# Feature-major products: all matmuls on a unit's high weights ahead of those on its low weights

## The chip, the cores and the metric

The kernel runs on one core of one Trainium2 chip. The metric is the device time of one execution in microseconds (us); the median of the runs counts. One core has TensorE (matrix products, called PE in the profile, its weight loads PEld), VectorE (DVE), ScalarE (ACT), GpSimd (POOL) and SyncE (SP, which here issues most transfers).

## The reference, cut to what matters

Two transformer layers follow one another on 256 tokens of 2048 features, all in float32.

```python
# first layer
proj = rmsnorm(x, norm_mix) @ w_in          # q, k, v of two attentions, and two gates
merged = sigmoid(ga) * (out_a @ w_branch_a) + sigmoid(gb) * (out_b @ w_branch_b)
x = x + merged @ w_out
u = rmsnorm(x, norm_ffn) @ w_up             # 2 x 5632 columns, then a convolution over three tokens
x = x + (silu(gate) * val) @ w_down
# second layer
h = rms_norm(x, g_norm) * (1 + scale) + shift
proj = h @ w_in_2                           # two more attentions, one with a choice of keys
x = x + gate * (concat([ya * silu(za), yb * silu(zb)]) @ w_out_2)
```

Nearly all of the arithmetic lies in the products with the weight matrices, some 395 MB of weights that are read once.

## The kernel before

A float32 product is made of three products in float32r, a shorter form of float32 that TensorE takes at a higher rate. Weights and activations are each split in two parts: `hi` is the value rounded to float32r and `lo` is what is left. The product is hi times hi, hi times lo and lo times hi.

**The stream of weights.** `Plan` writes down the order of all weight blocks. SP loads each block into a tile `raw`. A block is cut into units of 1024 numbers on each of the 128 partitions. For each unit ACT makes `wh` (high part, line 262) and DVE makes `wl` (low part, line 263), four buffers of each; `take` hands the next unit to a product and has the split of the unit three ahead put into the queues. `take` also lets the work beside the stream (`pump`: attention, norms, sums of finished products) put one step into the queues. The whole program is written out ahead of time; each engine works through its own queue in that order, and waits on semaphores where it needs another's result.

**Two kinds of product.** `gemm_tok` holds a tile of activations as TensorE's stationary matrix and streams a tile of weights, 512 columns (some 464 or 384) through it, lines 342 to 344: three matmuls of that width for each tile of 128 features and each half of the tokens. `gemm_feat` is the other way round: a tile of 128 x 128 weights is stationary and the activations of 256 tokens stream through. There `both` is the high and the low part of the activations side by side, 512 columns, so that one matmul on `wh` (line 368, here called wide) does two of the three products, and one on `wl` with the high part alone (line 369, 256 columns, called narrow) does the third. The left halves and the right halves of the result are added later (`sum_pair`, `grow`).

Each matmul has a weight load of its own in front of it, also where the stationary matrix is the same as before.

**Units in a feature-major product.** A unit holds four feature tiles of two column tiles each (f = 0, 1), or two feature tiles of four column tiles each. Both are eight pairs of a wide and a narrow matmul. A few products are made with `one=True`: there the low part of the activations is added in the same 256 columns, so that a unit is eight triples of 256-column matmuls, lines 365, 366 and 369. These are the first three chunks of the FFN's up product (8 + 4 + 4 units), the last chunk of its last down product (3 units) and the last chunk of the second layer's output product (4 units).

`ensure` is a hook that, before the tile k is used, has the instructions written that produce it, where a product starts while its activations are still being made.

Of the kernel before, what the change touches and what calls it, by code (L numbers as in the profile page):

```python
# [15 lines left out]
P = 128  # L16
# [26 lines left out]
class Paged:  # L43
    """A tensor of [128, 256] parts, four to a page; a page is taken at its first use."""

# [16 lines left out]
class Split:  # L62
    """A tensor of [128, 256] parts, each as two float32r parts side by side; two to a page."""

# [28 lines left out]
class Ahead:  # L93
    """Feature tiles built by a generator, per tiles at a step: a hook of a product over k, lead tiles ahead of it."""

# [17 lines left out]
class Plan:  # L113
    """The weights in the order in which they are used: blocks of [nk * 128, ncol], each one load, each cut into
    units of work."""

# [35 lines left out]
    def plan_ada(self, j):  # L152
        """128 columns of the modulation's matrix, turned: [columns, 2048]."""
        i = len(self.specs)
        self.block("w_ada_2", 0, 2, j, 1024)
        self.units.append((i, 0, 1, False))
        self.ada_half.append((i, 1, 1, True))
# [50 lines left out]
class Prog:  # L208
# [24 lines left out]

# [1 line left out]
    def issue_dma(self, upto):  # L235
# [41 lines left out]

# [1 line left out]
    def page(self, name, dtype=F32):  # L279
# [16 lines left out]

# [1 line left out]
    def pump(self):  # L298
# [28 lines left out]

# [1 line left out]
    def gemm_tok(self, a, nk, ncol, ensure=None):  # L329
        """[tokens, columns] as a tile [128, half, columns]."""  # L330
        nc = self.nc
        ps = self.mm()
        k = 0
        while k < nk:
            hv, lv, n = self.take(lambda: ensure(k) if ensure is not None else None)
            for j in range(n):
                if ensure is not None:
                    ensure(k)
                for t in range(2):
                    aH, aL = a(k, t)  # L340
                    o = ps[:, t, :ncol]
                    nc.tensor.matmul(o, aH, hv[:, j], start=(k == 0), stop=False)  # L342
                    nc.tensor.matmul(o, aH, lv[:, j], start=False, stop=False)  # L343
                    nc.tensor.matmul(o, aL, hv[:, j], start=False, stop=(k == nk - 1))  # L344
                k += 1
        return ps

    def gemm_feat(self, a, nk, ensure=None, nf=2, one=False):
        """[columns, tokens]; each pair of column tiles as (tile, tile) of [128, 512], to be summed by halves;
        one: summed already, in the first halves."""  # L350
        nc = self.nc
        mm = self.mm()
        ps = [mm[:, f] if f < 2 else self.sp() for f in range(nf)]
        k = 0
        while k < nk:
            hv, lv, n = self.take(lambda: ensure(k) if ensure is not None else None)
            for j in range(n):
                if ensure is not None:
                    ensure(k)
                both, hi, lo = a(k)  # L360
                for f in range(nf):
                    wH, wL = hv[:, j, f * P:(f + 1) * P], lv[:, j, f * P:(f + 1) * P]
                    first, last = k == 0, k == nk - 1
                    if one:
                        nc.tensor.matmul(ps[f][:, :256], wH, hi, start=first, stop=False)  # L365
                        nc.tensor.matmul(ps[f][:, :256], wH, lo, start=False, stop=False)  # L366
                    else:
                        nc.tensor.matmul(ps[f], wH, both, start=first, stop=False)  # L368
                    nc.tensor.matmul(ps[f][:, :256], wL, hi, start=False, stop=last)  # L369
                k += 1  # L370
        return [mm] + ([ps[2:]] if nf > 2 else [])

    def sum_pair(self, ps, out=None):
        """The sum of the two halves of the products of a pair; yields once, then the sum."""
        nc = self.nc
        lo = self.w2("lo").rearrange("p (f c) -> p f c", f=2)
        if isinstance(ps, list):
            for f in range(2):
                nc.scalar.copy(lo[:, f], ps[f][:, 256:])
        else:  # L380
            nc.scalar.copy(lo, ps[:, :, 256:])  # L381
        yield
        if out is None:
            out = lo
        if isinstance(ps, list):
            for f in range(2):
                nc.vector.tensor_tensor(out=out[:, f], in0=ps[f][:, :256], in1=lo[:, f], op=ALU.add)
        else:
            nc.vector.tensor_tensor(out=out, in0=ps[:, :, :256], in1=lo, op=ALU.add)
        yield out  # L390

# [1 line left out]
    def rsqrt_mean(self, out, ssq, n, width):  # L393
# [8 lines left out]

# [1 line left out]
    def load_x(self, g, steps=(4,), between=None):  # L404
# [14 lines left out]
    def square(self, i):  # L419
        """Squares of one pair of feature tiles, added up over the pairs; the last pair by itself."""  # L420
        nc = self.nc
        two = lambda t: t.rearrange("p (k c) -> p k c", k=2)
        if i == 0:
            nc.scalar.activation(two(self.ssum), self.xpair(0), AF.Square)
            return
        sq = self.w2("sqx")
        if i == 7:
            x = self.xpair(i)
            nc.scalar.activation(two(sq)[:, 0], x[:, 0], AF.Square)
            nc.vector.tensor_tensor(out=two(sq)[:, 1], in0=x[:, 1], in1=x[:, 1], op=ALU.mult)  # L430
            self.slast = sq
            return
        nc.scalar.activation(two(sq), self.xpair(i), AF.Square)  # L433
        nc.gpsimd.tensor_tensor(out=self.ssum, in0=self.ssum, in1=sq, op=ALU.add)  # L434
        if i == 6:
            nc.gpsimd.tensor_tensor(out=self.ssum[:, :256], in0=self.ssum[:, :256], in1=self.ssum[:, 256:], op=ALU.add)

    def token_sums(self, first):
        """Sums over the features of the squares of each token, [tokens, 1] for each half: all pairs but the last,
        then the last."""  # L440
        if first:
# [21 lines left out]
    def token_rstd(self):  # L463
        """1 / rms of each token: rtok [tokens, half] and rbc [every partition, token]."""
        self.token_sums(True)
# [23 lines left out]
    def build_raw(self, h, gain):  # L489
        """h = x * gain, without 1 / rms; yields after each feature tile."""  # L490
        for k in range(KD):
# [10 lines left out]
    def build_scaled(self, h, gain):  # L502
        """h = x * rstd * gain; yields after each pair of feature tiles."""
        nc = self.nc
# [11 lines left out]
    def build_shifted(self, h, gain, shift, r):  # L516
        """h = x * rstd * gain + shift; yields after each pair of feature tiles."""
        nc = self.nc
# [31 lines left out]
    def catch_up(self, gen, nk):  # L550
        """A hook of the product that reads what gen writes last, as its last two tiles."""
        def ensure(k):
# [6 lines left out]
    def grow(self, i, ps, h=None, gain=None, last=True, one=False):  # L559
        """x += product of one pair of feature tiles; squares summed and h = x * gain when it is the last addend."""  # L560
        nc = self.nc
# [22 lines left out]
    def heads(self, ps, t, runs, wait=0, rt=None):  # L584
        """One half of the tokens of one chunk: heads normed, turned, transposed; values copied.
        runs: (kind, first column, heads, destination, gain, rope)"""
        nc = self.nc
# [55 lines left out]
    def run_of(self, i, n, q, k, v, nq, nk, gq, gk, rq=None, rk=None, col=0):  # L643
        """Heads i .. i+n of the row q(nq) k(nk) v as runs; no run crosses a page."""
        out = []
# [28 lines left out]
    def attend(self, q, k, v, bias, emit, sink=None, causal=False):  # L674
        """softmax(q k + bias) v of one head, all queries; q, k: [d, tokens]; v(kt): [tokens, d].
        causal: the first half of the queries takes the first half of the keys only."""
        nc = self.nc
# [77 lines left out]

# [1 line left out]
    def ada_step(self, j, half, raw):  # L757
# [20 lines left out]

# [1 line left out]
    def run(self):  # L780
# [202 lines left out]
    def ffn(self):  # L983
# [17 lines left out]
        def conv_pair(ps, f, by):  # L1001
            """Yields between the engines; the last value is the pair of convolved tiles."""
            if by:
# [343 lines left out]
```

## Time and profile before

| what | value |
|---|---|
| time, median of 3 runs | 1910.98 us (1908.72 to 1911.16) |
| span of the profiled execution, first to last instruction | 1909.2 us |
| PE busy | 1890.8 us (99%) |
| DVE busy | 1372.0 us (72%) |
| ACT busy | 995.6 us (52%) |
| bytes moved | 399.07 MB, 209 GB/s on average |
| granted TensorE clock, mean of the span | 0.995 |

The profiled execution's own time is its span of 1909.2 us, which lies between the fastest and the slowest of the three runs. A granted clock of 1.00 is 2.4 GHz. Matmuls overlap at their ends: a matmul's duration in a row (0.40 us for a wide one) is longer than the time from its start to the next one's start, so pace is read from starts, or from counts in a stretch.

### The profile page before, as it was taken

What the parts mean: (1) busy time and instruction counts of PE and PEld (TensorE: products, weight loads), DVE (VectorE), ACT (ScalarE), POOL (GpSimd) and SP (SyncE); (2) the same over time, 40 slices, a digit from 0 to 9 for tenths busy, and PEclk for the clock granted to TensorE, in tenths of its full rate; (3) what the DMA queues carried; (4) which work ended last, traced back from release to release, by engine and by line L of the source; (5) the groups of instructions that cost most, each with busy time, mean ns of one, the idle gap of its engine ahead of it and who ended that gap; (6) DMA issues with size and microseconds to landing.
All of it is one profiled execution on the core that took longest, in us unless ns stands there. A gap on an engine that the chain in (4) does not pass through costs nothing.

```text
span 1909.2 us, 26942 instructions
## 1 busy us (share of the span) xinstructions
PE 1890.8 (99%) x10556; PEld 1639.9 (86%) x10556; DVE 1372.0 (72%) x2082; ACT 995.6 (52%) x1449; POOL 103.0 (5%) x87
## 2 busy tenths in 40 slices
PE   8999999999999999999999999999899999999999
PEld 6888888888888988888888888888788888898888
DVE  6888688677787877786777776666656855677664
ACT  6466555555454555533555434554454545666542
POOL 2111000000001300000000000000200100100000
PEclk9999999999999999999999999999899999999999
DMA  8665666666676466586555675454455455454562
GB/s 315 231 219 204 222 215 210 222 238 225 255 272 231 167 223 218 205 314 230 214 206 210 254 289 218 177 191 167 143 197 177 155 199 178 139 185 160 177 215 94
DMA packets 59231, 399.07 MB, mean 209 GB/s; under 512 B 6752, under 2 KB 7520, under 8 KB 14304
## 3 DMA queue, kind: packets, MB, share of 16 engines
q1 hardware_dynamic: 58176, 395.06, 57.4%
q0 software_dynamic: 640, 2.10, 0.3%
q8 instruction: 83, 1.36, 0.3%
q14 instruction: 44, 0.36, 0.0%
q10 hardware_dynamic: 288, 0.19, 0.0%
HBM read 395.22 MB, written 2.10 MB: 208 GB/s over the span
## 4 chain that ended last, share of the span: by engine, by line
PE 97%; DVE 2%; issue 1%; DMA 0%; ACT 0%; POOL 0%; SPq 0%; DVEq 0%; POOLq 0%; ACTq 0%
PE mm L368 42%; PE mm L369 22%; PE mm L342 8%; PE mm L344 8%; PE mm L343 8%; PE s L368 2%; PE s L369 1%; PE t L633 1%; PE t L730 1%; PE mm L365 1%; PE mm L366 1%; DVE h L485 1%; DVE wl L263 0%; DMA x<-in_x_dram 0%; PE t L750 0%
## 5 line engine op out<-in xcount | busy, mean ns | idle before, releaser
L263 DVE TENSOR_TENSOR wl<-raw,wh 128x1024 fp32r<-128x1024 f32 (+2 forms) x649 | 790.5, 1221 | 479.8 <-ACT wh L262 474.7
L262 ACT CAST wh<-raw 128x1024 fp32r<-128x1024 f32 (+2 forms) x649 | 675.1, 1042 | 662.9 <-PE mm L368 399.0
L368 PE MATMUL mm<-h,wh 128*128 128x512 f32 x2176 | 770.5, 398 | 0.0
L369 PE MATMUL mm<-h,wl 128*128 128x256 f32 x2272 | 638.0, 281 | 3.0 <-DVE wl L263 3.0
L368 PEld LDWEIGHTS mm<-h,wh 128*128 128x128 f32 x2176 | 408.8, 188 | 99.1
L369 PEld LDWEIGHTS mm<-h,wl 128*128 128x128 f32 x2272 | 429.4, 189 | 3.5 <-DVE wl L263 3.4
L342 PE MATMUL mm<-wh,h 128*128 128x512 f32 (+2 forms) x704 | 276.9, 393 | 5.0 <-DVE h L542 2.3
L344 PE MATMUL mm<-wh,h 128*128 128x512 f32 (+2 forms) x704 | 272.2, 387 | 3.1 <-DVE h L485 2.4
L343 PE MATMUL mm<-wl,h 128*128 128x512 f32 (+2 forms) x704 | 271.9, 386 | 0.0
L368 PE MATMUL mm<-g,wh 128*128 128x512 f32 x592 | 211.3, 399 | 0.0
L369 PE MATMUL mm<-g,wl 128*128 128x256 f32 x616 | 173.1, 281 | 0.0
L342 PEld LDWEIGHTS mm<-wh,h 128*128 128x128 f32 x704 | 134.6, 191 | 30.4 <-ACT wh L262 2.9
L344 PEld LDWEIGHTS mm<-wh,h 128*128 128x128 f32 x704 | 134.2, 191 | 29.7 <-DVE h L485 3.5
L343 PEld LDWEIGHTS mm<-wl,h 128*128 128x128 f32 x704 | 134.5, 191 | 22.7 <-DVE wl L263 0.6
L368 PEld LDWEIGHTS mm<-g,wh 128*128 128x128 f32 x592 | 111.2, 188 | 27.8
L759 DVE CUSTOM_DVE_ANT_0 raw<-raw,silu_c 128x1024 f32<-128x1024 f32 x96 | 119.2, 1242 | 0.0
L369 PEld LDWEIGHTS mm<-g,wl 128*128 128x128 f32 x616 | 116.4, 189 | 0.0
L381 ACT COPY lo<-mm 128x512 f32<-128x512 f32 x84 | 49.0, 584 | 62.9 <-PE mm L369 58.7
L434 POOL TENSOR_TENSOR ssum<-ssum,sqx 128x512 f32<-128x512 f32 x18 | 27.1, 1503 | 1015.1 <-ACT sqx L433 1014.9
L368 PE MATMUL mm<-m,wh 128*128 128x512 f32 x224 | 79.9, 399 | 0.0
L368 PE MATMUL mm<-y,wh 128*128 128x512 f32 x192 | 67.3, 394 | 0.0
L369 PE MATMUL mm<-m,wl 128*128 128x256 f32 x224 | 62.9, 281 | 0.0
(247 smaller groups left out, 2053.3 us busy)
## 6 DMA issues: line engine op xcount, KB each, us to landing
raw<-in_weights_dram SPq DMA_DIRECT2D x350, 1024.0 KB, 4.8
raw<-in_weights_dram SPq DMA_DIRECT2D x12, 768.0 KB, 4.3
raw<-in_weights_dram SPq DMA_DIRECT2D x11, 512.0 KB, 5.7
raw<-in_weights_dram SPq DMA_DIRECT2D x4, 928.0 KB, 4.6
x<-in_x_dram SPq DMA_DIRECT2D x6, 512.0 KB, 8.3
bias<-in_bias_b_dram POOLq DMA_DIRECT2D x8, 256.0 KB, 3.8
out_dram<-r SPq DMA_DIRECT2D x7, 256.0 KB, 2.0
silu_c<-in_c_dram SPq DMA_DIRECT2D x2, 512.0 KB, 7.4
```

The lines of the kernel that those rows point to most:

```text
L262: nc.scalar.copy(hv, rv)
L263: nc.vector.tensor_tensor(out=lv, in0=rv, in1=hv.bitcast(F32), op=ALU.subtract)
L342: nc.tensor.matmul(o, aH, hv[:, j], start=(k == 0), stop=False)
L343: nc.tensor.matmul(o, aH, lv[:, j], start=False, stop=False)
L344: nc.tensor.matmul(o, aL, hv[:, j], start=False, stop=(k == nk - 1))
L365: nc.tensor.matmul(ps[f][:, :256], wH, hi, start=first, stop=False)
L366: nc.tensor.matmul(ps[f][:, :256], wH, lo, start=False, stop=False)
L368: nc.tensor.matmul(ps[f], wH, both, start=first, stop=False)
L369: nc.tensor.matmul(ps[f][:, :256], wL, hi, start=False, stop=last)
L381: nc.scalar.copy(lo, ps[:, :, 256:])
L434: nc.gpsimd.tensor_tensor(out=self.ssum, in0=self.ssum, in1=sq, op=ALU.add)
L759: nc.vector.tensor_tensor_reduce(out=raw, in0=raw, in1=self.silu_c[half], scale=1.0, scalar=0.0, op0=ALU.mult, op1=ALU.add, accum_out=self ...
```

## The change

In `gemm_feat` the matmuls of a unit are regrouped. Before, a column tile's matmul on the high weights and that on its low weights follow each other, for each feature tile and column tile in turn. Now the loop over the unit's feature tiles does all matmuls on `hv` first, and a second loop does all matmuls on `lv`. The number of matmuls, their operands and their sums stay as they are (up to the order of addition). The hook `ensure(k + j)` of all tiles of a unit now comes before the first matmul on low weights. Lines further down the file move by five (368 becomes 370, 369 becomes 373, 365 and 366 become 367 and 368); apart from that only docstrings and comments differ.

```diff
             hv, lv, n = self.take(lambda: ensure(k) if ensure is not None else None)
+            parts = []
             for j in range(n):
                 if ensure is not None:
-                    ensure(k)
-                both, hi, lo = a(k)
+                    ensure(k + j)
+                parts.append(a(k + j))
+                both, hi, lo = parts[j]
                 for f in range(nf):
-                    wH, wL = hv[:, j, f * P:(f + 1) * P], lv[:, j, f * P:(f + 1) * P]
-                    first, last = k == 0, k == nk - 1
+                    wH = hv[:, j, f * P:(f + 1) * P]
+                    first = k + j == 0
                     if one:
                         nc.tensor.matmul(ps[f][:, :256], wH, hi, start=first, stop=False)
                         nc.tensor.matmul(ps[f][:, :256], wH, lo, start=False, stop=False)
                     else:
                         nc.tensor.matmul(ps[f], wH, both, start=first, stop=False)
-                    nc.tensor.matmul(ps[f][:, :256], wL, hi, start=False, stop=last)
-                k += 1
+            for j in range(n):
+                for f in range(nf):
+                    nc.tensor.matmul(ps[f][:, :256], lv[:, j, f * P:(f + 1) * P], parts[j][1], start=False,
+                                     stop=k + j == nk - 1)
+            k += n
```

**An ordinary unit.** This is TensorE's queue in one unit of the FFN's up product, before; `mm` is the result in PSUM, `h` the activations (two feature tiles to a page), and "waits" names the engines whose semaphores an instruction waits on (Activation is ACT). The unit goes on in this way to its sixteenth matmul.

```order
L368 MATMUL mm_6870<-h_6168,wh_6874 128x512 [waits Activation_49]
L369 MATMUL mm_6870<-h_6168,wl_6875 128x256 [waits DVE_49]
L368 MATMUL mm_6870<-h_6168,wh_6874 128x512
L369 MATMUL mm_6870<-h_6168,wl_6875 128x256
L368 MATMUL mm_6870<-h_6168,wh_6874 128x512
L369 MATMUL mm_6870<-h_6168,wl_6875 128x256
```

The same unit of the changed kernel, whole; x3 and x4 are so many instructions in a row that read alike.

```order
L370 MATMUL mm_6870<-h_6168,wh_6874 128x512 [waits Activation_49]
L370 MATMUL mm_6870<-h_6168,wh_6874 128x512 x3
L370 MATMUL mm_6870<-h_6208,wh_6874 128x512 x4
L373 MATMUL mm_6870<-h_6168,wl_6875 128x256 [waits DVE_49]
L373 MATMUL mm_6870<-h_6168,wl_6875 128x256 x3
L373 MATMUL mm_6870<-h_6208,wl_6875 128x256 x4
```

Eight wide matmuls now stand in a row and eight narrow ones behind them, and the first instruction that waits for `wl` has moved from the second place to the ninth.

**A unit of the products with one sum.** TensorE's queue at the second unit of the third chunk of the FFN's up product, before:

```order
L365 MATMUL mm_6128<-h_5228,wh_6061 128x256 [waits Activation_49]
L366 MATMUL mm_6128<-h_5228,wh_6061 128x256
L369 MATMUL mm_6128<-h_5228,wl_6062 128x256 [waits DVE_49]
L365 MATMUL mm_6128<-h_5228,wh_6061 128x256
L366 MATMUL mm_6128<-h_5228,wh_6061 128x256
L369 MATMUL mm_6128<-h_5228,wl_6062 128x256
```

The end of the same unit's matmuls on `wh` and its matmuls on `wl`, of the changed kernel (fourteen matmuls of lines 367 and 368 stand ahead of these rows):

```order
L367 MATMUL mm_6128<-h_5324,wh_6061 128x256
L368 MATMUL mm_6128<-h_5324,wh_6061 128x256
L373 MATMUL mm_6128<-h_5228,wl_6062 128x256 [waits DVE_49]
L373 MATMUL mm_6128<-h_5228,wl_6062 128x256 x3
L373 MATMUL mm_6128<-h_5324,wl_6062 128x256 x4
```

The wait for `wl` has moved from the unit's third matmul to its seventeenth.

## Rows read from the trace of the kernel before

**Rows 1.** The page's head, busy time, and slices.

```profile
span 1909.2 us, 26942 instructions
PE 1890.8 (99%) x10556; PEld 1639.9 (86%) x10556; DVE 1372.0 (72%) x2082; ACT 995.6 (52%) x1449; POOL 103.0 (5%) x87
...
PEclk9999999999999999999999999999899999999999
```

**Rows 2.** The page's chain that ended last, by engine and by line.

```profile
PE 97%; DVE 2%; issue 1%; DMA 0%; ACT 0%; POOL 0%; SPq 0%; DVEq 0%; POOLq 0%; ACTq 0%
PE mm L368 42%; PE mm L369 22%; PE mm L342 8%; PE mm L344 8%; PE mm L343 8%; PE s L368 2%; PE s L369 1%; PE t L633 1%; PE t L730 1%; PE mm L365 1%; PE mm L366 1%; DVE h L485 1%; DVE wl L263 0%; DMA x<-in_x_dram 0%; PE t L750 0%
```

**Rows 3.** The page's costliest groups: weight splits and token-major matmuls.

```profile
L263 DVE TENSOR_TENSOR wl<-raw,wh 128x1024 fp32r<-128x1024 f32 (+2 forms) x649 | 790.5, 1221 | 479.8 <-ACT wh L262 474.7
...
L342 PE MATMUL mm<-wh,h 128*128 128x512 f32 (+2 forms) x704 | 276.9, 393 | 5.0 <-DVE h L542 2.3
```

**Rows 4.** Windows, instructions of line 368 alone.

```profile
core 0: us, PE busy (x) PEld busy (x), PEclk, DMA share, GB/s
...
900.00:1000.00 100.00, 100.00 (x284) 53.18 (x283) 1.00 0.57 207
...
1800.00:1850.00 50.00, 50.00 (x145) 27.07 (x145) 1.00 0.58 206
1850.00:1910.00 60.00, 43.77 (x127) 23.55 (x126) 0.98 0.32 116
```

**Rows 5.** Timeline of PE, feature-major product at 900 us.

```profile
900.24 0.40 PE L368 MATMUL mm<-h,wh 128*128 128x512 f32 x1
900.47 0.28 PE L369 MATMUL mm<-h,wl 128*128 128x256 f32 x1
900.59 0.40 PE L368 MATMUL mm<-h,wh 128*128 128x512 f32 x1
900.83 0.28 PE L369 MATMUL mm<-h,wl 128*128 128x256 f32 x1
```

**Rows 6.** Timeline of PE, feature-major product at 1820 us.

```profile
1820.23 0.39 PE L368 MATMUL mm<-y,wh 128*128 128x512 f32 x1
...
1833.75 0.40 PE L368 MATMUL s<-y,wh 128*128 128x512 f32 x1
```

**Rows 7.** Timeline of PE, token-major product at 1578 us.

```profile
1578.20 0.39 PE L344 MATMUL mm<-wh,h 128*128 128x512 f32 x1
...
1582.96 0.39 PE L344 MATMUL mm<-wh,h 128*128 128x512 f32 x1
```

**Rows 8.** Timeline of PE, six attention matmuls within a token-major product.

```profile
129.99 0.39 PE L344 MATMUL mm<-wh,h 128*128 128x512 f32 x1
130.21 0.28 PE L748 MATMUL t<-pH,vs 128*128 128x256 f32 x1
130.33 0.28 PE L749 MATMUL t<-pL,vs 128*128 128x256 f32 x1
...
130.93 0.40 PE L342 MATMUL mm<-wh,h 128*128 128x512 f32 x1
131.16 0.40 PE L343 MATMUL mm<-wl,h 128*128 128x512 f32 x1
131.40 0.39 PE L344 MATMUL mm<-wh,h 128*128 128x512 f32 x1
...
132.31 0.39 PE L342 MATMUL mm<-wh,h 128*128 128x512 f32 x1
132.54 0.39 PE L343 MATMUL mm<-wl,h 128*128 128x512 f32 x1
```

**Rows 9.** Timeline of PE, one-sum product, line 369 alone.

```profile
643.62 0.39 PE L369 MATMUL mm<-h,wl 128*128 128x256 f32 x1 [0.54 <-DVE wl L263]
644.09 0.28 PE L369 MATMUL mm<-h,wl 128*128 128x256 f32 x1
...
646.25 0.28 PE L369 MATMUL mm<-h,wl 128*128 128x256 f32 x1
...
652.18 0.39 PE L369 MATMUL mm<-h,wl 128*128 128x256 f32 x1 [2.45 <-DVE wl L263]
```

**Rows 10.** Waits of PE: line, for whom, us in total, times, longest.

```profile
PE mm L369 <- DVE wl L263: 3.0, 2, 2.4
PE mm L344 <- DVE h L485: 2.4, 2, 2.0
```

**Rows 11.** Windows, all engines, around the one-sum products.

```profile
640.00:660.00 20.00, 17.02 (x139) 16.58 (x139) 19.65 (x32) 15.35 (x25) 4.73 (x3) 1.00 0.47 167
```

## Prediction

> **What bounds the kernel now.** I read the page's busy times first, then its chain of work that ended last, then the timeline of TensorE alone, and windows to see over how much of the span a pace holds. TensorE is busy for 99% of the span, no other engine for more than 72%, and the granted clock is 1.00 (2.4 GHz) but for one slice [rows 1]. The chain is 97% PE, and the two lines that the change regroups, 368 and 369, are 64% of it in the main tile alone [rows 2]. So TensorE sets the time, and the change can matter in two ways only: the pace at which TensorE starts its matmuls, and the few places where it waits.
>
> The pace, from start to start. In a feature-major product a wide matmul (512 columns) and its narrow one (256) take together 0.35 us: wide to narrow 0.23 or 0.24, narrow to wide 0.12 [rows 5]. A window says it more sharply: 283 weight loads of line 368 in 100 us, 353.4 ns a pair [rows 4]; I find 283 or 284 in each window of 100 us from 400 to 600 us and from 700 to 1300 us, of which one stands there. Near the end the same code runs at another pace: 39 pairs from 1820.23 to 1833.75, 346.7 ns a pair [rows 6], and so in the last two windows. So there are two paces of the same alternation, 6.7 ns apart.
>
> Now matmuls of one width in a row. Wide behind wide, in a token-major product: 21 steps in 1578.20 to 1582.96, 226.7 ns each [rows 7]. Narrow behind narrow, in the products with one sum: 18 steps in 644.09 to 646.25, 120.0 ns each [rows 9]. Their sum, 346.7, is the faster pace of the alternation. The slower pace is thus what the alternation adds, and it is what there is to win.
>
> One more reading, at which the trace comes nearest to the new order: a run of six narrow attention matmuls between wide ones [rows 8]. The first narrow one behind a wide one is followed after 0.12 us, like the others. But the wide ones behind the run do not fall at once into 0.227: the first starts at 130.93, the next at 131.16, 131.40, and only from 132.31 on do they run as in rows 7. From 129.99 to 132.54 there are eight wide and six narrow steps, 2.55 us; at 226.7 and 120.0 they would be 2.533. A run of narrow ones thus costs some 0.02 us, once, in the wide ones behind it (the rows are rounded to 0.01 us, so it is 0.01 to 0.03).
>
> **The change, part by part.** It adds and removes no instruction. The plan splits the weights in 649 units [rows 3]. A token-major unit has four matmuls of line 342 (the first two units of the program two each), so the 704 of them [rows 3] are 177 units, and 472 are feature-major. 23 of these are one-sum units (8 + 4 + 4 + 3 + 4), which leaves 449 ordinary units of eight pairs, 3592 pairs.
>
> 1. Ordinary units. After the change a unit is eight wide ones in a row and eight narrow ones in a row: 8 x 226.7 + 8 x 120.0 = 2.774 us, and 0.020 us for the way back from narrow to wide, 2.794 us. Before, it is 8 x 353.4 = 2.827 us at the slow pace and 2.774 us at the fast one. At the fast pace I count some 470 pairs: 271 in the windows from 1800 us on [rows 4], and I put the stretches around 250 to 350 us and 1700 to 1800 us, where the timeline changes between both paces, at 200. That makes 59 units at the fast pace and 390 at the slow one. Gain: 390 x 0.033 = 12.9 us; loss: 59 x 0.020 = 1.2 us; together 11.7 us less.
>
> That a wide one behind a wide one costs 226.7 ns in these products too is not in the trace, since no two stand together there. From below it is bounded by rows 7. From above the nearest row is the wide one of the slow alternation, 0.235 on average, 0.24 at most [rows 5]. I take the lower value: in the token-major product the stationary tile and the result's bank change too, at every third step, without a trace in the pace, and the wide ones there show the longer step only behind a narrow run [rows 8]. For the narrow run the rows of the one-sum products are the same operation on the same operands, with a new weight tile at every third; I take 120.0.
>
> The Trainium skill, in its page "TensorE: Matmul & The Clock Gate", sections "LDWEIGHTS (loading the stationary operand)" and "Back-to-back issue gap", speaks against any gain here: it gives a weight load 107 ns (128 columns at 1.2 GHz) and a matmul its columns at 2.4 GHz plus about 2.5 ns, with the next load pulled under the running matmul; a load then just hides behind a narrow matmul of 109 ns as behind a wide one, a pair is 325 ns in either order, and the sum of this step would be nothing. The trace agrees that loads lie under the matmul before, but its steps are some 11 ns longer, and their sum does depend on the neighbours.
>
> 2. One-sum units. All matmuls there have 256 columns and follow each other at 120.0 ns whichever line they are [rows 9], so regrouping them is worth nothing by pace. But two of the kernel's waits for `wl` lie here: 3.0 us [rows 10]. DVE is busy for 19.65 of the 20 us around them [rows 11], so what it makes comes no earlier; what changes is how much TensorE has to do before it needs it. TensorE is idle 0.54 us ahead of 643.62 and 2.45 us ahead of 652.18 [rows 9]. After the change fourteen more matmuls, 1.68 us, stand ahead of each of these waits. The first wait vanishes; TensorE then comes 0.5 us or a little more earlier to the second, has 1.68 us more to do there, and still waits some 1.5 us. What is gained at the end of it is those fourteen matmuls done: 1.7 us. I take it that no new wait follows: a split tile would have to come 1.9 us after TensorE has begun its unit.
>
> 3. Where it costs nothing. `wh` is read out 0.96 us earlier than before and `wl` at the same time, so ACT and DVE get their buffers back no later. `ensure` of a unit's later tiles comes earlier by up to four narrow matmuls, 0.5 us, where h is built just ahead of its use; no wait for such tiles shows in any feature-major product (the 2.4 us for h are in line 344, token-major [rows 10]), so cover is there; if it were gone in the one product built in this way, 0.5 us. The sums of squares in the middle of the last down chunk come 0.5 us earlier in TensorE's queue, and do not wait today. TensorE runs 0.7% faster than before against DVE, which has 28% to spare on average [rows 1].
>
> Sum: 11.7 + 1.7 = 13.4 us less. The profiled span is 1909.2 us, 1.8 us below the median of the runs, 1910.98; a gain made against the span is carried over to the median: 1897.6 us.
>
> **The rivals.**
>
> A, no way back to pay: the units fall into the faster pace, as the alternation does for long stretches [rows 6]. For it: there narrow and wide follow each other without any loss. Against it: rows 8. Then 390 x 0.053 + 1.7 = 22.4 us less, 1888.6 us.
>
> B, the order does nothing: each matmul in these products keeps its step, 353.4 for a pair, because of its own operands and not of its neighbour. For it: wide matmuls on `wh` have never been seen at 226.7 here. Against it: the same operands run at 346.7 a pair near the end [rows 6]. Only step 2 is left: 1909.3 us, no change that can be told; two versions of this kernel are told apart from about 0.2%, 3.8 us. The rule of the Trainium skill weighed above ends at the same time.
>
> C, slower: a wide matmul behind a wide one takes 0.236 here, as wide ones do on average in the slow alternation (0.23 and 0.24 [rows 5]), and narrow ones in a row 0.120. A pair is then 356 ns: 390 x 0.021 + 59 x 0.074 = 12.6 us more, less 1.7: 1921.9 us. For it: rows 8 show wide steps of 0.23 to 0.24 behind a run of narrow ones, and if the way back took all eight wide ones instead of six, the unit would never get out of it. Against it: the way back ends there after the sixth. It decides from a mean wide step of about 233 ns on; mine is 229.2 (226.7 + 20 / 8).
>
> **How the numbers follow.** My forecast has 0.60: 1897.6 us, with a way back of 0.005 to 0.035 us a unit 1891 to 1904 us. A has 0.14, B 0.14, C 0.10; 0.02 is for anything else. The range of eight in ten takes in the forecast, A and B, and leaves C out: 1887 to 1910 us. Faster by over 0.2%: the forecast, A and a little of the rest, 0.76; within 0.2%: 0.14; slower: 0.10.
>
> **What would show it.** In the changed profile the timeline of an ordinary unit must show wide starts some 0.233, 0.236, 0.228 apart at first and 0.227 from the seventh on, and narrow starts 0.12 apart, a unit every 2.79 us. In windows of 100 us in the FFN line 370 should have 286 loads where line 368 had 283; between 1800 and 1850 us it should have fewer than 145. Wide steps of 0.227 from the first on are A; 0.233 or more in all eight are C; a unit of 2.83 us is B. Of the waits for `wl` one should be left, of some 1.5 us, with TensorE at its seventeenth matmul of that unit. The prediction fails if wide ones in a row pay more than 233 ns for operands that rows 7 do not have, or if a wait that is not in rows 10 grows where TensorE now runs ahead.

## The result, and the profile after

The changed kernel takes 1896.9 us (median of 4 runs, 1895.17 to 1897.08) where the kernel before takes 1911.07 us (4 runs, 1908.72 to 1912.82). The ratio is 0.9925, with a 95% interval of 0.9913 to 0.9937: 14.2 us less. The prediction was 1897.6 us, 13.4 us less.

The page of the changed kernel, its head and busy times, which answer to [rows 1]:

```profile
span 1893.4 us, 26939 instructions
PE 1877.2 (99%) x10556; PEld 1642.1 (87%) x10556; DVE 1370.1 (72%) x2082; ACT 993.3 (52%) x1449; POOL 105.5 (6%) x87
```

As many instructions on TensorE, 15.8 us less of span (one execution each), and TensorE still busy for 99%: the gain is in its pace. The profiled execution took 1895.17 us, the fastest of the four. Its span is 1.8 us shorter than that, since the span runs from the first to the last instruction; so the span of 1909.2 us of the kernel before stands for a run of about 1911 us, its median, and not for one of 1909.2.

The timeline of PE at 900 us, lines 370 (wide) and 373 (narrow), answers to [rows 5]; instructions of one kind in a row are merged, so a row is a whole run, and its count stands at the end:

```profile
902.01 2.00 PE L370 MATMUL mm<-h,wh 128*128 128x512 f32 x8
903.86 1.11 PE L373 MATMUL mm<-h,wl 128*128 128x256 f32 x8
904.81 2.00 PE L370 MATMUL mm<-h,wh 128*128 128x512 f32 x8
...
957.88 2.00 PE L370 MATMUL mm<-h,wh 128*128 128x512 f32 x8
```

From 902.01 to 957.88 are twenty units, 2.794 us each; 2.794 was forecast, and the alternation had 2.827. From the first narrow start to the next wide one are 0.952 us, 0.008 less than eight steps of 120.0 ns: the first step is 113 ns, the others 119 or 120. The wide run takes 1.841 us, 0.027 more than eight steps of 226.7 ns, so the unit pays 20 ns. (Steps to the ns are differences of starts in the trace; the rows shown are rounded to 0.01 us.) Where in the run the excess lies shows in two narrower windows of the same view, whose rows begin at the first and at the fifth wide matmul:

```profile
902.01 0.86 PE L370 MATMUL mm<-h,wh 128*128 128x512 f32 x3
...
902.95 0.85 PE L370 MATMUL mm<-h,wh 128*128 128x512 f32 x3
```

The first four steps take 0.930 us by the trace's starts (0.907 at 226.7), the other four 0.911. One by one the wide steps are 233, 236, 228, 232 or 233, 231, and 227 from the sixth on. The trace before has the same steps, to 1 ns, behind the six narrow ones of [rows 8]: the way back that stood there once is now in every unit.

At the end of the program, where the alternation ran at its faster pace [rows 6], the same order costs more than before:

```profile
1822.05 2.00 PE L370 MATMUL mm<-y,wh 128*128 128x512 f32 x8
...
1838.81 2.00 PE L370 MATMUL mm<-y,wh 128*128 128x512 f32 x8
```

Six units at 2.793 us, where eight pairs at 346.7 ns are 2.774.

The windows of line 370 alone, to be held against [rows 4]:

```profile
900.00:1000.00 100.00, 71.55 (x287) 51.35 (x286) 1.00 0.60 221
...
1800.00:1850.00 50.00, 35.78 (x145) 25.66 (x144) 1.00 0.56 204
```

286 wide weight loads in 100 us, 283 before; 144 in the late window, 145 before. Of PE's waits for `wl` [rows 10] one is left:

```profile
PE mm L373 <- DVE wl L263: 1.1, 1, 1.1
```

Read from the starts of the two traces, the time of each stretch from its first matmul to that of the next one (us; the first row counts from the start of the span, the last to the start of the last matmul):

| stretch | before | after |
|---|---|---|
| start and token-major products of layer 1 | 233.4 | 231.9 |
| ordinary units of layer 1 up to the FFN | 376.1 | 372.6 |
| one-sum units of the first three up chunks | 51.2 | 49.0 |
| ordinary units of the FFN | 692.5 | 684.4 |
| one-sum units of the last down chunk, first product of layer 2 | 42.9 | 42.4 |
| queries of the index (ordinary units) | 45.9 | 45.5 |
| token-major products of layer 2 | 275.7 | 275.7 |
| ordinary units at the end | 176.0 | 176.5 |
| last one-sum units | 11.4 | 11.4 |

The four stretches of ordinary units give 3.5 + 8.1 + 0.4 - 0.5 = 11.5 us (11.6 before rounding), the first one-sum units 2.2 us. The rest of the 15.8 us, 2.0 us, lies in the first row and in the fifth. The first row, 1.5 us, is a stretch that the change does not touch, and there the two traces differ in the granted clock. All engines, the kernel before:

```profile
26.00:30.00 4.00, 4.00 (x14) 3.33 (x13) 4.00 (x8) 2.18 (x5) 0.00 (x0) 0.57 0.99 408
```

The changed kernel:

```profile
26.00:30.00 4.00, 4.00 (x25) 3.49 (x24) 4.00 (x8) 2.06 (x3) 0.00 (x0) 1.00 0.94 385
```

The mean granted clock of these 4 us is 0.57 in the one, part of it at 1.2 GHz, and 1.00 in the other (TensorE had been busy for 3.69 and 4.01 of the 6 us ahead of it). A clock of 0.43 less over 4 us makes 1.7 us, about the 1.5 us of the row; that it is the cause is worked out and was not tested. It belongs to these two executions and not to the change. What the change does, 11.6 + 2.2 = 13.8 us, fits the 14.2 us between the medians, and single runs of the kernel before lie up to 4 us apart.

### The profile page after: what moved, and what is told of

It reads as the page before. It is cut to its first block, busy times and chain, and to the rows that moved or that the text cites. A ratio compares the mean times of both kernels' runs of the same rounds, so it can differ in the third digit from the quotient of the medians.

```text
span 1893.4 us, 26939 instructions
## 1 busy us (share of the span) xinstructions
PE 1877.2 (99%) x10556; PEld 1642.1 (87%) x10556; DVE 1370.1 (72%) x2082; ACT 993.3 (52%) x1449; POOL 105.5 (6%) x87
## 4 chain that ended last, share of the span: by engine, by line
PE 97%; DVE 2%; ACT 0%; DMA 0%; issue 0%; POOL 0%; SPq 0%; DVEq 0%; ACTq 0%
PE mm L370 42%; PE mm L373 22%; PE mm L342 8%; PE mm L344 8%; PE mm L343 8%; PE s L370 2%; PE s L373 1%; PE mm L367 1%; PE mm L368 1%; PE t L638 1%; DVE h L490 1%; PE t L735 1%; DVE wl L263 1%; PE t L755 0%; PE s L700 0%; PE s L699 0%
## 5 line engine op out<-in xcount | busy, mean ns | idle before, releaser
L370 PE MATMUL mm<-h,wh 128*128 128x512 f32 x2176 | 546.2, 393 | 0.0
L370 PEld LDWEIGHTS mm<-h,wh 128*128 128x128 f32 x2176 | 391.2, 189 | 69.9
L373 PEld LDWEIGHTS mm<-h,wl 128*128 128x128 f32 x2272 | 310.0, 190 | 22.6 <-DVE wl L263 1.3
L373 PE MATMUL mm<-h,wl 128*128 128x256 f32 x2272 | 318.9, 282 | 1.1 <-DVE wl L263 1.1
L370 PE MATMUL mm<-g,wh 128*128 128x512 f32 x592 | 153.7, 392 | 0.0
L373 PEld LDWEIGHTS mm<-g,wl 128*128 128x128 f32 x616 | 87.0, 190 | 6.6
L373 PE MATMUL mm<-g,wl 128*128 128x256 f32 x616 | 91.2, 282 | 0.0
L1024 ACT ACTIVATE c<-lo,conv 128x256 f32<-128x256 f32 x80 | 43.8, 595 | 37.6 <-DVE lo L394 37.6
L402 POOL TENSOR_TENSOR rstdh<-ms,mhalf 128x4 f32<-128x4 f32 (+3 forms) x32 | 40.8, 1291 | 396.5 <-DVE ms L401 396.5
L370 PE MATMUL mm<-m,wh 128*128 128x512 f32 x224 | 58.1, 392 | 0.0
```

Of the source, the lines that this page charges most:

```text
L373: nc.tensor.matmul(ps[f][:, :256], lv[:, j, f * P:(f + 1) * P], parts[j][1], start=False, stop=k + j == nk - 1)
L402: nc.gpsimd.tensor_tensor(out=out, in0=ms, in1=self.mhalf[:, :width], op=ALU.pow)
L1024: nc.scalar.activation(c[:, i], u[:, i], AF.Identity, scale=w[:, 1:2], bias=w[:, 3:4])
```

## Experiments

The theory is that of the prediction: wide behind wide steps at 226.7 ns, narrow behind narrow at 120, the slower pace of the alternation is what the change saves, and each way back from narrow to wide costs some 20 ns; one-sum units gain by a later wait. The runs below take the two terms apart, vary the length of the runs, the width of the narrow matmul, and the pace of the alternation. Each was timed beside the kernel before on the same chip.

**One half of the change at a time.** Only the one-sum units regrouped:

```diff
+                    late.append((j, f))
+                    if len(late) == (8 if one else 1):
+                        for i, e in late:
+                            nc.tensor.matmul(ps[e][:, :256], lv[:, i, e * P:(e + 1) * P], parts[i][1], start=False,
+                                             stop=k + i == nk - 1)
+                        late = []
```

> Ordinary units in turn as before, only the 23 one-sum units regrouped. Theory (there the gain is that the wait for wl stands fourteen matmuls later): of the two waits for wl, 3.0 us, one of about 1.1 to 1.6 us is left, all else as before, 1909.3 us, 1.7 us less, too little to be told by the time alone; ordinary pairs at 353 ns, 283 wide weight loads in 100 us. Rival (the one-sum units have no part in the gain): waits of 3.0 us as before and 1911 us. Should the alternation fall into its faster pace after the regrouped chunks, it would be up to 13 us less, and 288 loads in 100 us.

Median 1908.41 us, ratio 0.9972 (0.9954 to 0.9990). But the twelve runs fall in two groups: nine from 1907.95 to 1910.27, three from 1895.20 to 1896.03. The profile is of the first group:

```profile
PE mm L374 <- DVE wl L263: 2.2, 2, 1.1
```

The waits for `wl` (us in total, times, longest) are down from 3.0 to 2.2 us, and the windows have 283 wide loads in 100 us, as before. The first one-sum units take 49.0 us, as in the changed kernel, with one wait of 1.1 us left in them. The other wait is new and was not expected. It lies in the first ordinary unit of the FFN, which TensorE now reaches sooner:

```profile
662.21 0.39 PE L374 MATMUL mm<-h,wl 128*128 128x256 f32 x1 [1.11 <-DVE wl L263]
```

In the changed kernel no wait shows there: eight wide matmuls stand ahead of the unit's first one on `wl`. In this half alone the new wait takes back 1.1 of the 2.2 us. The nine runs are 1 to 3 us below the kernel before, as forecast. The three are some 13 us lower than the nine, what the expectation put on the case that the alternation falls into its faster pace; they were not profiled, so for them this is argued and not shown.

Only the ordinary units regrouped (in the same lines, `1 if one else 8`):

> The other half of the change alone: ordinary units regrouped, the 23 one-sum units in turn. Theory (the two terms of the prediction stand by themselves, 11.7 us for the pace of the ordinary units and 1.7 us for the later wait): 1.7 to 2.2 us more than the changed kernel, about 1898.9 us, ratio to before 0.9935; waits for wl of 3.0 us as before. Rival (the terms are not independent, TensorE loses again elsewhere what the faster units give it): 1901 us or more, with new or longer waits.

1898.68 us, ratio 0.9934 (0.9922 to 0.9947), waits for `wl` of 3.0 us. The ordinary units alone give 12.4 us, and the changed kernel is 1.8 us below it, about the other term. To within the spread of single runs, 2 us to either side here, the two terms add up in the changed kernel; they are not independent, as the new wait in the other half shows.

**Length of the runs.** The same lines with a limit of 4, and with one of 2, for ordinary units:

> The changed kernel, but in ordinary units four wide matmuls and then their four narrow ones, twice a unit (one-sum units as in the changed kernel). Theory (a narrow run leaves something behind that the wide ones after it walk off step by step, in the same steps whatever comes later): wide steps 233, 236, 228, 233 ns and narrow steps 113, 120, 120, 120, a unit of 2 x 1403 = 2806 ns against 2794; 449 units x 12 ns = 5.4 us more than the changed kernel, 1902.5 us. Rival 1 (a fixed toll of 20 ns for every change from narrow to wide): 2774 + 40 = 2814 ns a unit, 1906 us. Rival 2 (any run longer than one is as good as eight): 1897 us.

> The same with two wide ones and their two narrow ones, four times a unit. Theory (steps walked off): wide steps 233, 236 and narrow steps 113, 120, a unit of 4 x 702 = 2808 ns, 1903.5 us, so hardly more than runs of four. Rival 1 (fixed toll of 20 ns for every change): 2774 + 80 = 2854 ns a unit, 27 ns more than the slow alternation, about 1924 us, slower than the kernel before. Rival 2 (any run is as good as eight): 1897 us.

Runs of four: 1902.22 us, ratio 0.9952 (0.9939 to 0.9965). Runs of two: 1894.82 us, 0.9913 (0.9900 to 0.9926). The timeline of PE, runs of four, sixteen units from the first row to the last:

```profile
900.85 1.09 PE L370 MATMUL mm<-h,wh 128*128 128x512 f32 x4
...
945.76 1.09 PE L370 MATMUL mm<-h,wh 128*128 128x512 f32 x4
```

Runs of two, 64 pairs:

```profile
900.08 0.63 PE L370 MATMUL mm<-h,wh 128*128 128x512 f32 x2
...
922.37 0.63 PE L370 MATMUL mm<-h,wh 128*128 128x512 f32 x2
```

Runs of four take 2.807 us a unit, the theory's sum (2.806), and neither the fixed toll nor the absence of one. But the steps are not those that the theory lists. By the starts there are two kinds of run, in turn: one has wide steps of 235, 234, 236 and 224 ns and narrow ones of 117 and three times 120, the next has about the theory's wide steps (234, 235, 229 and 232) and narrow ones of 118, 119, 117 and 117. No narrow run begins with 113. That the sum agrees is luck. Runs of two take 348.3 ns a pair, 2.786 us a unit, less than runs of eight: here all three expectations are wrong. The theory had the narrow steps at 113 and 120; in the trace they are 115 or 116 and 112 or 113 in one run, 113 or 114 and 119 in the next. So what a change of width costs isn't a sum of fixed steps behind each change. Runs of the same length differ in turn, and the cost is not even ordered by the length of the run: 53 ns a unit for one (slower pace), 13 for two, 33 for four, 20 for eight. For each way back from narrow to wide that is 7, 3, 17 and 20 ns.

**Longer runs.** Every second unit takes its low weights first, so that runs of sixteen arise:

```diff
+            if turn:
+                low(False)
...
+            if not turn:
+                low(True)
+            turn = not turn and not one
```

> The changed kernel, but every second unit of an ordinary product takes its low weights first, so that runs are sixteen narrow and sixteen wide. Theory (about 20 ns once for each way back from narrow to wide, whatever the length of the runs): 20 ns for two units instead of one, 449 x 10 ns = 4.5 us less than the changed kernel, 1892.4 us, ratio to before 0.990; wide steps 227 from the seventh to the sixteenth. Rival 1 (what a narrow run leaves grows with its length): 40 ns after sixteen, no change, 1897 us. Rival 2 (the low weights, needed eight matmuls earlier than in the changed kernel, come late): waits of TensorE for wl in many units, 1900 us or more.

1893.05 us, ratio 0.9903 (0.9891 to 0.9916), the lowest median here, 1.8 us below runs of two. In the timeline, from one wide run to the fourth behind it:

```profile
902.64 3.82 PE L379 MATMUL mm<-h,wh 128*128 128x512 f32 x16
...
924.90 3.82 PE L379 MATMUL mm<-h,wh 128*128 128x512 f32 x16
```

Eight units in 22.26 us, 2.783 us each, 2.784 expected. At eight and at sixteen the toll is 20 ns once for each change and has not grown with the run; wide steps are 227 ns from the sixth to the sixteenth. The second rival is right in one place only, the first turned unit of the FFN, behind the crowded one-sum chunks:

```profile
645.50 1.21 PE L366 MATMUL mm<-h,wl 128*128 128x256 f32 x8 [0.81 <-DVE wl L263]
...
656.64 1.22 PE L366 MATMUL mm<-h,wl 128*128 128x256 f32 x8 [1.38 <-DVE wl L263]
```

The first of these waits is in a one-sum unit, the second, 1.38 us, is the turned unit's. No other turned unit waits.

**Is it the weight load?** The matmuls on low weights of ordinary units made wider, 288 and 384 columns:

```diff
-                    nc.tensor.matmul(ps[f][:, :256], lv[:, j, f * P:(f + 1) * P], parts[j][1], start=False,
-                                     stop=k + j == nk - 1)
+                    m = 256 if one else 288
+                    nc.tensor.matmul(ps[f][:, :m], lv[:, j, f * P:(f + 1) * P],
+                                     parts[j][1] if one else parts[j][0][:, :m], start=False, stop=k + j == nk - 1)
```

> The changed kernel, with the matmuls on the low weights of ordinary units 288 columns wide instead of 256 (they take in 32 columns of the low activations, so that a small term is added that the other kernels leave out). Theory (the toll comes from a narrow matmul being hardly longer than the load of the weights behind it: 120 ns beside some 118): with steps of 133 ns there is room for the load, no toll, all wide steps 227 ns from the first on; a unit of 8 x 226.7 + 8 x 133.3 = 2880 ns, 449 x 87 = 39 us more, 1936 us. Rival (the toll comes with any change of width): wide steps of 233, 236, 228, 233 behind the run as in the changed kernel, 2900 ns a unit, 1945 us.

> The same with 384 columns (128 columns of the low activations more). Theory (room for the load): narrow steps 173.3, wide steps 226.7 from the first on, a unit of 3200 ns, 449 x 406 = 182 us more than the changed kernel, 2079 us. Rival (any change of width): 3220 ns a unit, 2088 us.

1945.14 us and 2107.91 us, one run each. The timeline of PE with 288 columns, nineteen units between the rows:

```profile
902.71 2.01 PE L370 MATMUL mm<-h,wh 128*128 128x512 f32 x8
...
957.87 2.02 PE L370 MATMUL mm<-h,wh 128*128 128x512 f32 x8
```

With 384 columns, sixteen units between the rows:

```profile
903.16 2.01 PE L370 MATMUL mm<-g,wh 128*128 128x512 f32 x8
...
955.43 2.01 PE L370 MATMUL mm<-g,wh 128*128 128x512 f32 x8
```

With 288 columns a unit takes 2.903 us, where steps of 226.7 and 133.3 make 2.880: a toll of 23 ns, and the rival's time. The rival's steps are not there, though: wide steps lie between 224 and 236 ns up to the eighth, 232 on average. With 384 columns a unit takes 3.267 us, where 226.7 and 173.3 make 3.200: the toll is not gone, it is 67 ns, three times that of 256 columns, and both expectations are wrong. So the explanation by the room for the next weight load falls in the form that was tried, with a load of some 118 ns. No row shows a load of that length: by [rows 4] 283 loads are busy for 53.18 us, 188 ns each, longer than each of the three narrow steps, and a narrow step longer than that was not tried. What the runs show is a toll at each of the three widths. In the one-sum units before, where `wh` and `wl` follow each other at one width, the steps are 120.0 ns without one [rows 9]. Why it differs between widths stays open.

**The pace of the alternation.** The kernel before, with four transposes of 128 columns ahead of two products (of the two calls the one in the FFN is shown):

```diff
+    def nudge(self):
+        pt = self.tp()
+        for i in range(4):
+            self.nc.tensor.transpose(pt[:, i * P:(i + 1) * P], self.ident, self.ident)
...
+                if n_chunk == self.DEFER:
+                    self.nudge()
                 ps = self.gemm_feat((raw if by else h).both, KD, ensure=ens, nf=n, one=by)
```

> The kernel before, its order in turn untouched, with four transposes of 128 columns (results unused) ahead of two products: the second one of the stage with the two branches, near 337 us, and the first one of the FFN in ordinary units, near 655 us. Theory (the alternation has two paces, 353.3 and 346.7 ns a pair, and keeps the one that it falls into at its start; behind four transposes it falls into the faster one): both stretches run at 346.7, 288 wide weight loads in 100 us from 400 to 600 and from 700 to 1300 us, some 2730 pairs x 6.7 ns = 18 us less, 0.9 us more for the transposes, 1894 us; 1898 to 1899 us if only the longer stretch takes it, 1907 us if only the first. Rival (the pace drifts back to the slower one within some products): 283 loads again and 1911 to 1912 us.

1898.85 us, ratio 0.9940 (0.9928 to 0.9951), all five runs within 2 us. Windows of line 368 alone:

```profile
400.00:500.00 100.00, 100.00 (x284) 53.18 (x284) 1.00 0.62 226
700.00:800.00 100.00, 100.00 (x289) 53.89 (x289) 1.00 0.59 215
...
1100.00:1200.00 100.00, 100.00 (x289) 53.87 (x289) 1.00 0.65 237
```

The longer stretch took the faster pace and kept it for 680 us, the first one did not: 1898 to 1899 was the forecast for that case. The order of the matmuls in these products is the old one to the last instruction. So much of what the change gains is there without it, 11.6 us against the kernel before: one and the same order has two paces, and with other matmuls ahead of it the other one came.

The same with the one-sum units regrouped:

> The one-sum units regrouped, ordinary units in turn, and the same two groups of four transposes. Theory (both gains add up): the 1894 us of the transposes alone less the 1.7 us that the later wait for wl is worth, 1892 us, about the kernel with turned units. Rival (the faster pace is a matter of chance at every entry): single runs near 1892, 1897, 1905 and 1910 us.

1896.46 us, ratio 0.9939 (0.9923 to 0.9955): ten of twelve runs from 1894.80 to 1899.28, two at 1908.70 and 1910.33. The profiled run has 289 loads from 700 us on and 284 from 400 us, as the run before it. The 1892 us of the theory were not reached, since the first stretch again did not take the faster pace; the ten runs are about 3 us below the transposes alone, so the two gains go together where the faster pace is caught. Two of twelve runs lie where the slower pace would put them; they were not profiled.

**Both together.** Turned units everywhere, but in the FFN ordinary units in turn behind four transposes:

```diff
+            plain = self.in_turn and not one
...
+                    if plain:
+                        nc.tensor.matmul(ps[f][:, :256], lv[:, j, f * P:(f + 1) * P], hi, start=False,
+                                         stop=k + j == nk - 1)
```

> One-sum units as in the changed kernel; ordinary units of the FFN in turn behind four transposes; all other ordinary units turned as in the run with turned units. Theory (in turn at the faster pace a pair costs 346.7 ns and no toll, 684 us down to 680 us for the FFN's stretch): 4 us less than with turned units alone, about 1889.5 us. Rival (behind the regrouped one-sum units the alternation takes the slower pace): 283 wide weight loads in 100 us from 700 us on, 13 us more, about 1902 us, in some runs or in all.

1903.82 us, ratio 0.9962 (0.9948 to 0.9975): the rival. The timeline of PE shows how the pace was lost:

```profile
654.90 0.39 PE L381 MATMUL mm<-h,wh 128*128 128x512 f32 x1
655.13 0.28 PE L383 MATMUL mm<-h,wl 128*128 128x256 f32 x1
655.25 0.39 PE L381 MATMUL mm<-h,wh 128*128 128x512 f32 x1
656.35 0.39 PE L383 MATMUL mm<-h,wl 128*128 128x256 f32 x1 [0.72 <-DVE wl L264]
656.58 0.39 PE L381 MATMUL mm<-h,wh 128*128 128x512 f32 x1
```

Up to 655.25 a pair takes 0.35 us at the faster pace (seven pairs from 652.82, 347 ns each); then TensorE waits 0.72 us for `wl`, and from there on the windows have 284 loads in 100 us, the slower pace. But the run before, with regrouped one-sum units and transposes, has the same wait at the same matmul, in the ninth pair behind its transposes:

```profile
660.64 0.39 PE L370 MATMUL mm<-h,wh 128*128 128x512 f32 x1
661.75 0.38 PE L374 MATMUL mm<-h,wl 128*128 128x256 f32 x1 [0.72 <-DVE wl L263]
661.97 0.40 PE L370 MATMUL mm<-h,wh 128*128 128x512 f32 x1
```

Its windows of line 370 have the faster pace behind it:

```profile
700.00:800.00 100.00, 100.00 (x290) 54.02 (x289) 1.00 0.60 218
```

So the pace changed at the wait in the one run and not in the other, with the same matmuls and the same wait just ahead (further ahead, in the first layer, the ordinary units are turned in the one and in turn in the other). The transposes were then put two products later, behind that wait:

> As the run before (turned units, and in the FFN ordinary units in turn behind four transposes), but transposes and alternation begin two products later, behind the place where TensorE waited 0.72 us for wl. Theory (the faster pace was entered, and it was this wait that threw the alternation into the slower one): with no wait behind the transposes 289 wide weight loads in 100 us from 700 us on, about 3.8 us less than with turned units alone, 1889.3 us. Rival (behind regrouped one-sum units or turned ones the alternation does not hold the faster pace whatever waits): 284 loads again, about 1903 us.

1904.19 us, ratio 0.9962 (0.9949 to 0.9976), 283 and 284 loads in all windows from 700 us on, with no wait behind the transposes: the rival again. Here the pace is the slower one from the first pairs behind the transposes on. So four transposes do not secure the faster pace, and neither does the absence of a wait; that the wait ended it in the run before is not shown.

## Why the prediction was right

The step that carried it was the reading of pace by neighbours, 226.7 ns for wide behind wide and 120.0 for narrow behind narrow. Both came out in the new order as read, on operands on which they had not been seen together: wide steps from the sixth of a run on, narrow ones from the third; rivals B and C, which made the operands the cause, are refuted by the 2.794 us of a unit.

The second step, the 20 ns for the way back taken from one place in a token-major product [rows 8], kept the forecast from ending at rival A, 1888.6 us. It was measured in each unit at the same size, also where it is a loss: the last ordinary stretch became 0.5 us longer. For the ordinary units 11.7 us were forecast; 11.6 us lie in their stretches, and 12.4 us in the run with these units alone. Some luck is in this step. The place in [rows 8] has a run of six narrow ones, and the forecast took its toll for a run of eight without a reason why it should be the same; runs of two and four later paid 3 and 17 ns for the same way back.

The third, the later wait for `wl` in the one-sum units, was put at 1.7 us; the stretch gives 2.2 us and the difference to the run with ordinary units alone 1.8 us. The wait that is left is 1.1 us. The prediction had 1.5, though its own terms, 2.45 + 0.54 - 1.68, make 1.3. What it had wrong is that DVE's tile comes no earlier. The split that ends the wait, before and after:

```profile
650.91 1.22 DVE L263 TENSOR_TENSOR wl<-raw,wh 128x1024 fp32r<-128x1024 f32 x1
```

```profile
645.33 1.22 DVE L263 TENSOR_TENSOR wl<-raw,wh 128x1024 fp32r<-128x1024 f32 x1
```

The one-sum units begin at 609.48 and 604.46 us, so the split starts 41.43 us into them before and 40.87 after, 0.56 us sooner. With the fourteen matmuls, 1.68 us, that makes the 2.2 us. DVE is busy without a break ahead of the split, but more than 20 us earlier in the stretch it waits for `wh`, and ACT in turn for TensorE to release a buffer of `wh`. An ACT row of before and of after, 5.89 and 5.05 us into the stretch:

```profile
615.37 1.05 ACT L262 CAST wh<-raw 128x1024 fp32r<-128x1024 f32 x1 [1.84 <-PE s L366]
```

```profile
609.51 1.05 ACT L262 CAST wh<-raw 128x1024 fp32r<-128x1024 f32 x1 [1.25 <-PE s L368]
```

`wh` is released earlier, as the prediction said in its third part, and that was left out of its second. No wait in ordinary feature-major units grew in the changed kernel, as was claimed for the places that cost nothing. That no new wait would follow holds for the whole change only: with the one-sum units alone one of 1.1 us came up.

What the forecast took for a property of the order is not one of the order alone. The alternation has the faster pace too, and the runs with transposes got it with the old order. The slower pace was what was there to win, as said, but the regrouping is one way to it among others, and not the best: turned units halve the toll.

The Trainium skill, page "TensorE: Matmul & The Clock Gate", section "Back-to-back issue gap", has a matmul taken by itself at its columns over 2.4 GHz plus 2.5 ns, which is 215.8 ns for 512 columns and 109.2 for 256. The section sets this apart from a stream of weight loads and matmuls, to which the prediction applied it. At a granted clock of 1.00 the runs here have 226.7 and 120.0 ns among neighbours of one width, and other steps where widths change.

## What to carry to other kernels

Where TensorE is the bound, count starts, not durations, and compare the step of a matmul among its like with its step in the mix: the difference, here 6.7 ns in 353, is what an order can win over the pairs that run at the slower pace, some 3100 of 3592 by the prediction's count. Look in the old trace for a place that already has the new order by chance, with its way in and out; its cost per change of kind goes into the sum, with a range where the place has runs of another length. Where a matmul releases a buffer earlier, follow that buffer through the engines that fill it, also on stretches well ahead of the wait. If a regrouping helps, try to turn every second group before making anything more elaborate: the number of changes is halved with the same buffers. Here it won 3.9 us more, with one new wait of 1.4 us.

## What was not expected of the hardware

One order of instructions, with no wait in it, ran at 353.3 or at 346.7 ns a pair for hundreds of microseconds, and the matmuls just ahead do not settle which: behind four transposes it was the faster in the FFN and the slower in the first stretch of the same run. In one kernel, one-sum units alone regrouped, executions of the same program lay 13 us apart. Two runs with the same matmuls, the same four transposes and the same wait of 0.72 us just ahead went on at different paces. What decides was not found. The excess of runs of two, four, eight and sixteen, 13, 33, 20 and 10 ns a unit, follows no rule that was proposed, nor does that of 384 columns.

In the profile of the kernel before with transposes, the wait of 2.4 us for `wl` in the one-sum units was followed by a stretch of lower granted clock (1.2 GHz in part), 0.91 on average of this window of all engines, where [rows 11] has 1.00 behind a wait as long:

```profile
640.00:660.00 20.00, 17.03 (x128) 16.58 (x128) 19.64 (x33) 15.33 (x25) 4.12 (x3) 0.91 0.47 172
```

In that stretch 256 columns step at 0.21 us instead of 0.12. The lower clock is not what brought the faster pace behind it: with the one-sum units regrouped too the same window has 1.00, and the faster pace came as well. The longest wait for `wl` in the changed kernel is 1.1 us, and the window's clock there 1.00; whether the shorter wait keeps the clock up in more executions was not tried.
